# Four column blocks of one input product made in one pass, in a one-core decoder trunk kernel

## The chip, the core and the metric

The kernel runs on one core of a Trainium2 chip. The metric is the device time of one execution in microseconds. Engines are named as the profile names them: PE (TensorE, matmuls), PEld (its weight loads), DVE (VectorE), ACT (ScalarE), POOL (GpSimd), SP (the queue that issues the DMAs).

## What is computed

One layer of a hybrid decoder trunk on 256 positions of width 2048, float32. Around the change only its first part matters: the normalized input times slices of `w_in`, and the compression of two of these slices.

```python
h = rms_norm(x, norm_mix[l])
z = h @ w_in[l]
z_a, z_b, z_cq, z_ckv_c, z_ckv_s, z_ckv_w, z_cg = jnp.split(z, split_at, axis=-1)
...
blocks = jnp.concatenate([sub[:, :, :-1], sub[:, :, 1:]], axis=3) + pos
h = jax.nn.gelu(blocks.reshape(bsz, ng, n_c, CMP_LEN * hd) @ w1)
return h @ w2
```

`z_ckv_c` (512 columns, keys and values to be compressed) and the keys in `z_ckv_s` and `z_ckv_w` (256 each) are the four column blocks of 256 that the change is about. Behind this part come the attentions, an output product, cross attention over a memory, and a squared-ReLU MLP that takes over half of the time.

## The kernel before, in words

Every float32 operand of a large product is split into a high part (rounded to float32r by ScalarE, `split` L82) and a low part (the remainder, by VectorE, L83), and a product is three products of parts. `products_t` (L155 to 175) does one block, 512 rows of the contraction by 256 columns: 8 matmuls of 512 columns (the high weights by both parts of x, L164) and 8 of 256 columns (the low weights by the high part of x, L169). `gemm_t` does a whole product of 256 columns in four such blocks, each with its load, its split and its matmuls. Its sum takes two of the eight PSUM banks; `join` (L191 to 196) adds its two halves on ScalarE and VectorE.

Weights come from memory into five `raw` buffers, all over the one SP queue. The split weights stand in three buffers `wh` and three `wl`, which all products share, the compression's too. PSUM is two pools of four banks each: `pacc` (two sums) and `pmisc`. The rows of an engine run in their order in the program; that order is set by a scheduler when the program is built, which starts from the order in the code.

The order in the code: the first product (`cmps`, L240 to 265) makes both column blocks of `z_ckv_c` together: x comes in pieces, is multiplied by the gains and split (`put_act`, into `hx`), and each block of x meets two weight blocks. Then comes k0 (the selected keys) as a `gemm_t` of its own, with the generator `squares` between its blocks, which joins the first product and sums the squares of x. From that sum come `rx` (the row scale: `mean_eps`, `rstd`; matmul `pss`, L117, POOL's power, L123) and `rxb`, the same along the free axis (`along_free`, matmul `psb`, L133, copy L134). The joined first product (`kraw`, in `cw`) is multiplied by `rxb` (L313), and the generator `compress` (L328 to 371) adds the position term (L330), splits the result into `blk`, and runs `ph`, 64 small matmuls (L340 to 343) in four blocks for the keys, then as many for the values. It is advanced between the blocks of k1 (the window keys) and of sg (`gemm`, 8 blocks of 12 matmuls of 280 columns, L212). Then come wv, cq and the rest.

## Time and profile before

| | |
|---|---|
| runs | 1197.72, 1197.37, 1196.21 us; median 1197.37 |
| profiled execution | 1196.66 us, of which 1194.9 are the span from the first to the last instruction |
| mean granted TensorE clock | 0.999 |
| PE, DVE, ACT, POOL busy | 1178.7, 741.2, 590.4, 12.0 us |
| memory traffic | 224.24 MB, 188 GB/s in the mean |

A row of the timeline gives the start, the busy time, the engine, the line of the code, the operation, the tiles written and read, their shape, and how many like ones follow each other; in brackets stands the idle time before it and what ended it. Matmuls overlap their neighbours' ends, so of two rows of PE the difference of the starts tells the pace, not the busy time.

### The profile page before, as it was taken

What the parts mean: (1) busy time and instruction counts of PE and PEld (TensorE: products, weight loads), DVE (VectorE), ACT (ScalarE), POOL (GpSimd) and SP (SyncE); (2) the same over time, 40 slices, a digit from 0 to 9 for tenths busy, and PEclk for the clock granted to TensorE, in tenths of its full rate; (3) what the DMA queues carried; (4) which work ended last, traced back from release to release, by engine and by line L of the source; (5) the groups of instructions that cost most, each with busy time, mean ns of one, the idle gap of its engine ahead of it and who ended that gap; (6) DMA issues with size and microseconds to landing.
All of it is one profiled execution on the core that took longest, in us unless ns stands there. A gap on an engine that the chain in (4) does not pass through costs nothing.

```text
span 1194.9 us, 16486 instructions
## 1 busy us (share of the span) xinstructions
PE 1178.7 (99%) x6450; PEld 1016.8 (85%) x6450; DVE 741.2 (62%) x938; ACT 590.4 (49%) x812; POOL 12.0 (1%) x18
## 2 busy tenths in 40 slices
PE   8999999999999999999999999999999999999996
PEld 6898888888888889888888888888888888888885
DVE  7875876569776567665545565545566445656554
ACT  7564555466544467544433444433444333444443
POOL 0000000000000000000000000000000000000000
PEclk9999999999999999999999999999999999999999
DMA  8676444557555554555565565556665656565553
GB/s 297 225 256 186 132 124 140 179 183 229 181 190 193 180 174 160 178 192 189 193 192 192 188 190 193 191 193 192 190 189 182 202 193 197 178 193 193 193 179 106
DMA packets 65673, 224.24 MB, mean 188 GB/s; under 512 B 7995, under 2 KB 9531, under 8 KB 65467
## 3 DMA queue, kind: packets, MB, share of 16 engines
q1 hardware_dynamic: 65307, 222.14, 57.6%
q8 instruction: 50, 0.82, 0.3%
q10 hardware_dynamic: 288, 1.05, 0.3%
q14 instruction: 28, 0.23, 0.1%
HBM read 221.06 MB, written 2.10 MB: 187 GB/s over the span
## 4 chain that ended last, share of the span: by engine, by line
PE 96%; DVE 1%; issue 1%; ACT 1%; DMA 1%; SPq 0%; POOLq 0%; POOL 0%; DVEq 0%; ACTq 0%
PE dn L212 27%; PE up L164 20%; PE up L169 10%; PE wo L164 5%; PE cq L164 3%; PE wo L169 2%; PE xo L153 2%; PE v L212 2%; PE bv L212 2%; PE mv L212 2%; PE cmp L164 1%; PE k L164 1%; PE cq L169 1%; PE bq L164 1%; PE xq L164 1%; PE mk L164 1%
## 5 line engine op out<-in xcount | busy, mean ns | idle before, releaser
L83 DVE TENSOR_TENSOR wl<-raw,wh 128x1024 fp32r<-128x1024 f32 (+3 forms) x414 | 496.4, 1201 | 332.2 <-ACT wh L82 329.8
L82 ACT ACTIVATE wh<-raw 128x1024 fp32r<-128x1024 f32 (+3 forms) x414 | 429.0, 1038 | 432.2 <-PE dn L212 185.5
L164 PE MATMUL up<-h,wh 128*128 128x512 f32 x1024 | 316.9, 395 | 0.0
L212 PE MATMUL dn<-wh,hid 128*128 128x512 f32 x992 | 306.2, 389 | 0.0
L169 PEld LDWEIGHTS up<-h,wl 128*128 128x128 f32 x1024 | 187.6, 188 | 42.2
L212 PEld LDWEIGHTS dn<-wh,hid 128*128 128x128 f32 x992 | 186.2, 188 | 38.7
L169 PE MATMUL up<-h,wl 128*128 128x256 f32 x1024 | 197.0, 279 | 0.0
L212 PE MATMUL dn<-wl,hid 128*128 128x512 f32 x496 | 193.3, 390 | 1.1 <-DVE wl L83 0.6
L164 PEld LDWEIGHTS up<-h,wh 128*128 128x128 f32 x1024 | 158.4, 189 | 2.7
L212 PEld LDWEIGHTS dn<-wl,hid 128*128 128x128 f32 x496 | 93.1, 188 | 21.4 <-DVE wl L83 2.2
L164 PE MATMUL wo<-mix,wh 128*128 128x512 f32 x256 | 79.1, 395 | 0.0
L169 PEld LDWEIGHTS wo<-mix,wl 128*128 128x128 f32 x256 | 46.5, 188 | 10.3
L193 ACT ACTIVATE half<-up 128x512 f32<-128x512 f32 x32 | 19.2, 599 | 63.6 <-PE up L164 63.6
L195 DVE TENSOR_TENSOR half<-up,half 128x512 f32<-128x512 f32 x32 | 22.2, 693 | 43.5 <-ACT half L193 43.5
L169 PE MATMUL wo<-mix,wl 128*128 128x256 f32 x256 | 49.0, 279 | 0.0
L164 PE MATMUL cq<-hx,wh 128*128 128x512 f32 x128 | 40.4, 396 | 0.0
L164 PEld LDWEIGHTS wo<-mix,wh 128*128 128x128 f32 x256 | 39.7, 189 | 0.8
L667 DVE SCALAR_TENSOR_TENSOR xt<-dn,m,xt 128x512 f32<-128x512 f32 (+1 forms) x34 | 22.9, 715 | 14.5 <-PE dn L212 14.5
L82 ACT ACTIVATE hid<-half 128x512 fp32r<-128x512 f32 x32 | 20.2, 633 | 16.6 <-DVE half L718 16.6
L169 PEld LDWEIGHTS cq<-hx,wl 128*128 128x128 f32 x128 | 23.5, 188 | 5.1
L164 PE MATMUL cmp<-hx,wh 128*128 128x512 f32 x64 | 21.8, 439 | 5.6 <-ACT wh L82 5.6
L169 PE MATMUL cq<-hx,wl 128*128 128x256 f32 x128 | 25.7, 281 | 0.0
(283 smaller groups left out, 1277.3 us busy)
## 6 DMA issues: line engine op xcount, KB each, us to landing
raw<-in_w_up SPq DMA_DIRECT2D x128, 512.0 KB, 4.3
raw<-in_w_down SPq DMA_DIRECT2D x128, 512.0 KB, 4.4
raw<-in_w_t SPq DMA_DIRECT2D x52, 512.0 KB, 4.0
raw<-in_w_out SPq DMA_DIRECT2D x32, 512.0 KB, 3.8
raw<-in_w_bv SPq DMA_DIRECT2D x8, 512.0 KB, 3.7
raw<-in_w_v SPq DMA_DIRECT2D x8, 512.0 KB, 3.7
raw<-in_w_mk SPq DMA_DIRECT2D x8, 512.0 KB, 4.3
raw<-in_w_q SPq DMA_DIRECT2D x8, 512.0 KB, 4.3
```

The costliest lines, as they stand in the source:

```text
L82: nc.scalar.activation(hi, src, AF.Copy)
L83: nc.vector.tensor_tensor(lo, src, f32(hi), op=ALU.subtract)
L153: nc.tensor.matmul(acc[:, f, 0, :], w[:, kk, fs], x[:, kk, l, :], start=(kk == 0 and j == 0), stop=(kk == 3 and j == 2))
L164: nc.tensor.matmul(acc[:, f].rearrange("p a s -> p (a s)"), wh[:, kk, f * P:(f + 1) * P], xk, start=start, stop=stop)
L169: nc.tensor.matmul(acc[:, f, 0, :], wl[:, kk, f * P:(f + 1) * P], x[:, kk, 0, :], start=False, stop=False)
L193: nc.scalar.activation(lo, acc[:, :, 1, :], AF.Copy)
L195: nc.vector.tensor_tensor(d, acc[:, :, 0, :], lo, op=ALU.add)
L212: nc.tensor.matmul(acc[t][:, :n], lhs[k // 4][:, k % 4, l, ts], w[:, kk, :], start=(k == 0 and j == 0), stop=(k == KD - 1 and j == 2))
L667: nc.vector.scalar_tensor_tensor(xs, acc[t][:, cs], r3[:, t:t + 1], xs, op0=ALU.mult, op1=ALU.add)
```

## The change

All four column blocks are made in one pass over x, in four sums that fill the eight PSUM banks (a pool `first`, closed before `pmisc` and `pacc` are opened). For the first block of x three weight blocks come in pieces beside x's pieces and the fourth whole; for the other three blocks of x the four weight blocks come whole, one after the other. The squares of x lie between them. All four sums are joined behind the last product; `rx`, `rxb` and the compression follow there. There is no product k1 beside which the compression could run: `cgen` is now advanced between the blocks of sg, wv and, if anything were left, cq. The PSUM pools get `reuse_waits="tile"`: a new tile waits for the earlier tiles in its own banks, not for the whole earlier pool.

```diff
--- before.py
+++ after.py
@@ -48,8 +48,6 @@
     wp = ctx.enter_context(tc.tile_pool(name="wp", bufs=3))
     ap = ctx.enter_context(tc.tile_pool(name="ap", bufs=4))
     sp = ctx.enter_context(tc.tile_pool(name="sp", bufs=2))
-    pacc = ctx.enter_context(tc.tile_pool(name="pacc", bufs=2, space=PSUM))
-    pmisc = ctx.enter_context(tc.tile_pool(name="pmisc", bufs=2, space=PSUM))
 
     def f32(t):
         return t.bitcast(F32)
@@ -237,32 +235,6 @@
 
     hx = new_act("hA", "hx")
 
-    cmps = [pacc.tile([P, 2, 2, S], F32, tag="acc", name=f"cmp{m}") for m in range(2)]
-    for b in range(4):
-        ws = []
-        for m in range(2):
-            raw = wp.tile([P, 1024], F32, tag="raw", bufs=5, name="raw")
-            wh = wp.tile([P, 1024], F32R, tag="wh", name="wh")
-            wl = wp.tile([P, 1024], F32R, tag="wl", name="wl")
-            ws.append((raw, wh, wl))
-        i = 0
-        for step in ((1, 1, 2), (2, 2), (4,), (4,))[b]:
-            k = 4 * b + i
-            cs = slice(i * 256, (i + step) * 256)
-            for m, (raw, wh, wl) in enumerate(ws):
-                if m == 0:
-                    nc.sync.dma_start(xres[:, k:k + step, :],
-                                      a["xT"][b].rearrange("p (k s) -> p k s", k=4)[:, i:i + step, :])
-                    if k == 0:
-                        nc.sync.dma_start(gT, a["gT"])
-                loads.append(nc.sync.dma_start(raw[:, cs], a["w_t"][CMP + m, b][:, cs]))
-                if m == 0:
-                    put_act(hx, k, xres[:, k:k + step, :], 0)
-                split(wh[:, cs], wl[:, cs], raw[:, cs])
-            i += step
-        for m, (raw, wh, wl) in enumerate(ws):
-            products_t(cmps[m], hx[b], wh.rearrange("p (k n) -> p k n", k=4), wl.rearrange("p (k n) -> p k n", k=4),
-                       b == 0, b == 3)
     C = {}
 
     def consts(them):
@@ -272,27 +244,68 @@
             with tc.issue_after(loads[-1].ins):
                 nc.sync.dma_start(C[name], a[name].partition_broadcast(P) if name == "bs" else a[name])
 
-    consts([("ident", [P, P]), ("posT", [P, LCMP]), ("sel", [2 * M2, M2]), ("hmask", [P, 4]), ("rowv", [P, 2])])
-    ident = C["ident"]
-
     cw = slot("hC", "cw", F32).rearrange("p k a s -> p (k a s)")
     kraw = cw[:, :4 * S].rearrange("p (g s) -> p g s", g=4)
+    ssq = sp.tile([P, 2, S], F32, tag="ssq", name="ssq")
+
+    with tc.tile_pool(name="first", bufs=1, space=PSUM, reuse_waits="tile") as pfirst:
+        accs = [pfirst.tile([P, 2, 2, S], F32, tag=f"a{m}", name=f"cmp{m}" if m < 2 else f"k{m - 2}") for m in range(4)]
+        cols = [CMP, CMP + 1, KV, KV + 1]
+
+        def load_x(k, n):
+            b = k // 4
+            nc.sync.dma_start(xres[:, k:k + n, :],
+                              a["xT"][b].rearrange("p (k s) -> p k s", k=4)[:, k % 4:k % 4 + n, :])
+
+        def load_w(m, b, raw, cs):
+            loads.append(nc.sync.dma_start(raw[:, cs], a["w_t"][cols[m], b][:, cs]))
+
+        def add_block(m, b, w):
+            products_t(accs[m], hx[b], *(t.rearrange("p (k n) -> p k n", k=4) for t in w), b == 0, b == 3)
+
+        ws = [[wp.tile([P, 1024], F32, tag="raw", bufs=5, name="raw")]
+              + [wp.tile([P, 1024], F32R, tag=n, name=n) for n in ("wh", "wl")] for m in range(3)]
+        k = 0
+        for n in (1, 1, 2):
+            cs = slice(k * 256, (k + n) * 256)
+            load_x(k, n)
+            if k == 0:
+                nc.sync.dma_start(gT, a["gT"])
+            for m in range(3):
+                load_w(m, 0, ws[m][0], cs)
+                if m == 0:
+                    put_act(hx, k, xres[:, k:k + n, :], 0)
+                raw, wh, wl = ws[m]
+                split(wh[:, cs], wl[:, cs], raw[:, cs])
+            k += n
+        for m in range(3):
+            add_block(m, 0, ws[m][1:])
+        w = split_w(load_raw(a["w_t"][cols[3], 0]))
+        add_block(3, 0, w)
+        for b in range(1, 4):
+            for i in range(2):
+                load_x(4 * b + 2 * i, 2)
+                put_act(hx, 4 * b + 2 * i, xres[:, 4 * b + 2 * i:4 * b + 2 * i + 2, :], 0)
+            for m in range(4):
+                w = split_w(load_raw(a["w_t"][cols[m], b]))
+                add_block(m, b, w)
+                for n in {1: (0, None, 1, None), 2: (2, None, 3, None), 3: (4, 5, 6, 7)}[b][m:m + 1]:
+                    if n is not None:
+                        add_squares(ssq, xres[:, 2 * n:2 * n + 2, :], n == 0)
+            if b == 2:
+                consts([("ident", [P, P]), ("posT", [P, LCMP]), ("sel", [2 * M2, M2]), ("hmask", [P, 4]), ("rowv", [P, 2])])
+                ident = C["ident"]
+        k01 = []
+        for m in range(4):
+            j = join(accs[m], "first", kraw[:, 2 * m:2 * m + 2, :] if m < 2 else None)
+            if m >= 2:
+                k01.append(j)
+    pmisc = ctx.enter_context(tc.tile_pool(name="pmisc", bufs=2, space=PSUM, reuse_waits="tile"))
+    pacc = ctx.enter_context(tc.tile_pool(name="pacc", bufs=2, space=PSUM, reuse_waits="tile"))
     vs = slot("hC", "vs", F32).rearrange("p k a s -> p (k a s)")
     vcat = vs[:, :1024].rearrange("p (b t n) -> p b t n", b=2, t=2)
     zb = vs[:, 1024:].rearrange("p (t n) -> p t n", t=2)
     kcat = slot("hB", "kcat").rearrange("p (g a) b s -> p g a b s", g=2)
-    ssq = sp.tile([P, 2, S], F32, tag="ssq", name="ssq")
-
-    def squares():
-
-        for m, acc in enumerate(cmps):
-            join(acc, "cmp", kraw[:, 2 * m:2 * m + 2, :])
-        for b in range(4):
-            for n in (2 * b, 2 * b + 1):
-                add_squares(ssq, xres[:, 2 * n:2 * n + 2, :], n == 0)
-            yield
-
-    acc_k0 = gemm_t(hx, a["w_t"][KV], "k0", between=squares())
     rx = rstd(mean_eps(ssq, "mx"), "rx")
     rxb = along_free(rx, "rxb")
     rq = cp.tile([P, 2], F32, name="rq")
@@ -302,8 +315,8 @@
     consts([("cau", [P, S]), ("mcmp", [P, 2, NCMP]), ("mB", [P, 384]), ("bs", [P, NB]), ("triu", [P, P])])
     cau, mB, mcmp = C["cau"], C["mB"], C["mcmp"]
 
-    def join_split(acc, hi, lo, name, rb=None):
-        j = join(acc, name)
+    def join_split(acc, hi, lo, name, rb=None, joined=False):
+        j = acc if joined else join(acc, name)
         if rb is not None:
             nc.vector.tensor_tensor(j, j, rb[:, None, :].to_broadcast([P, 2, S]), op=ALU.mult)
         split(hi, lo, j)
@@ -311,7 +324,8 @@
     for m in range(2):
         km = kraw[:, 2 * m:2 * m + 2, :]
         nc.vector.tensor_tensor(km, km, rxb[:, None, :].to_broadcast([P, 2, S]), op=ALU.mult)
-    join_split(acc_k0, kcat[:, :, 0, 0, :], kcat[:, :, 1, 0, :], "k0", rxb)
+    for g in range(2):
+        join_split(k01[g], kcat[:, :, 0, g, :], kcat[:, :, 1, g, :], f"k{g}", rxb, joined=True)
 
 
 
@@ -371,9 +385,6 @@
             yield
 
     cgen = compress()
-    acc = gemm_t(hx, a["w_t"][KV + 1], "k1", between=cgen)
-    join_split(acc, kcat[:, :, 0, 1, :], kcat[:, :, 1, 1, :], "k1", rxb)
-
 
     gate = cp.tile([P, 2, 8, 3], F32, name="gate")
     acc = gemm(hx, a["w_sg"], 2, NG, "sg", between=cgen)
@@ -386,9 +397,7 @@
 
     nc.vector.tensor_tensor(gate[:, :, :, 0], gate[:, :, :, 0], C["rowv"][:, :, None].to_broadcast([P, 2, 8]),
                             op=ALU.mult)
-    for _ in cgen:
-        pass
-    acc = gemm(hx, a["w_wv"], 4, S, "wv")
+    acc = gemm(hx, a["w_wv"], 4, S, "wv", between=cgen)
     for t in range(2):
         nc.scalar.activation(vcat[:, 1, t, :], acc[t][:, :S], AF.Copy, scale=rx[:, t:t + 1])
 
@@ -436,8 +445,10 @@
         qT = slot(("hB", "hC")[g], f"q{g}")
         mix[2 + g] = slot("hB", f"mix{2 + g}")
         for m in range(2):
-            acc = gemm_t(hx, a["w_t"][CQ + 2 * g + m], f"cq{g}{m}")
+            acc = gemm_t(hx, a["w_t"][CQ + 2 * g + m], f"cq{g}{m}", between=cgen)
             join_split(acc, qT[:, 2 * m:2 * m + 2, 0, :], qT[:, 2 * m:2 * m + 2, 1, :], "q")
+        for _ in cgen:
+            pass
 
         psc = pmisc.tile([P, 2, 4, 2, NCMP], F32, tag="sc", name="psc")
         for t in range(2):
```

TensorE's order changes only up to the first cq product; behind it its rows are the same. TensorE where the compression begins, before (`k_494` is k1, `ph` the compression, `hx_80` the first block of x):

```order
L164 MATMUL k_494<-hx_80,wh 128x512 x2
L169 MATMUL k_494<-hx_80,wl 128x256 x2
L340 MATMUL ph<-wh,blk 60x128
L341 MATMUL ph<-wl,blk 30x128 x2
L343 MATMUL ph<-wh,blk 60x128
L341 MATMUL ph<-wl,blk 30x128
L343 MATMUL ph<-wh,blk 60x128
L341 MATMUL ph<-wl,blk 30x128
```

The first `ph` stands behind one block of k1, and k1's next block follows after 15 more matmuls of `ph`. TensorE now, at the end of the four products (`k_86` is k1):

```order
L162 MATMUL k_86<-hx_77,wh 128x512 x2
L115 MATMUL pss<-ones,ssq 128x1 x2
L210 MATMUL sg<-wh,hx_74 128x280
L210 MATMUL sg<-wl,hx_74 128x280
L210 MATMUL sg<-wh,hx_74 128x280 x2
```

`pss`, which stood inside the first product, is behind the last one, and sg's 24 matmuls on `hx_74`, two blocks, follow. TensorE after these 24, up to the first `ph` (`hx_75` is the second block of x):

```order
L131 MATMUL psb<-dg,ones 128x128 x2
L210 MATMUL sg<-wh,hx_75 128x280
L210 MATMUL sg<-wl,hx_75 128x280
L210 MATMUL sg<-wh,hx_75 128x280 x2
L210 MATMUL sg<-wl,hx_75 128x280
L210 MATMUL sg<-wh,hx_75 128x280 x2
L210 MATMUL sg<-wl,hx_75 128x280
L210 MATMUL sg<-wh,hx_75 128x280 x2
L210 MATMUL sg<-wl,hx_75 128x280
L210 MATMUL sg<-wh,hx_75 128x280
L354 MATMUL ph<-wh,blk 60x128
L355 MATMUL ph<-wl,blk 30x128 x2
```

After the third sg block 48 `ph` matmuls stand in one piece, and the fourth sg block behind them. VectorE from the row scale to `blk`, before:

```order
L132 TENSOR_SCALAR dg<-ident,rx 128x128 x2
L299 TENSOR_SCALAR rq<-rx 128x2
L301 TENSOR_SCALAR nrx<-rx 128x2
L83 TENSOR_TENSOR wl<-raw,wh 128x1024
L195 TENSOR_TENSOR cw<-cmp_85,half 128x512
L83 TENSOR_TENSOR wl<-raw,wh 128x1024 x2
L313 TENSOR_TENSOR cw<-cw,rxb 128x512 x2
L330 TENSOR_TENSOR cw<-cw,posT 128x32x15 x2
L83 TENSOR_TENSOR wl<-raw,wh 128x1024
L83 TENSOR_TENSOR blk<-cw,blk 128x32x30
L83 TENSOR_TENSOR wl<-raw,wh 128x1024
```

VectorE at the same place now:

```order
L116 TENSOR_SCALAR mx<-pss 128x2
L130 TENSOR_SCALAR dg<-ident,rx 128x128 x2
L312 TENSOR_SCALAR rq<-rx 128x2
L314 TENSOR_SCALAR nrx<-rx 128x2
L81 TENSOR_TENSOR wl<-raw,wh 128x1024
L81 TENSOR_TENSOR wl<-raw,wh 128x560
L326 TENSOR_TENSOR cw<-cw,rxb 128x512 x2
L321 TENSOR_TENSOR half<-half,rxb 128x512 x2
L344 TENSOR_TENSOR cw<-cw,posT 128x32x15 x2
L81 TENSOR_TENSOR wl<-raw,wh 128x1024
L81 TENSOR_TENSOR kcat<-half,kcat 128x2x256 x2
L81 TENSOR_TENSOR blk<-cw,blk 128x32x30
```

The scaling of two k blocks (L321) and two low parts of `kcat` are new between `dg` and the low part of `blk` (the last row); of four `wl` of 1024 columns and a join, two `wl` of 1024 and one of 560 are left there. On ScalarE two table loads are added, one before the values' gelu and one before the first exponential of the attentions.

## Rows read from the trace of the kernel before

**Rows 1.** The page, busy time of TensorE, its share of the span, instructions.
```profile
PE 1178.7 (99%) x6450; PEld 1016.8 (85%) x6450; DVE 741.2 (62%) x938; ACT 590.4 (49%) x812; POOL 12.0 (1%) x18
```

**Rows 2.** The page, chain that ended last, shares by engine.
```profile
PE 96%; DVE 1%; issue 1%; ACT 1%; DMA 1%; SPq 0%; POOLq 0%; POOL 0%; DVEq 0%; ACTq 0%
```

**Rows 3.** TensorE's waits, whole span: us in total, times, longest.
```profile
PE cmp L164 <- ACT wh L82: 5.6, 3, 4.4
PE ox L651 <- DVE oT L83: 0.7, 1, 0.7
```

**Rows 4.** Timeline of PE in the first product.
```profile
4.44 2.08 PE L164 MATMUL cmp<-hx,wh 128*128 128x512 f32 x4 [4.44 <-ACT wh L82]
...
6.31 1.06 PE L169 MATMUL cmp<-hx,wl 128*128 128x256 f32 x4
...
12.25 0.62 PE L164 MATMUL cmp<-hx,wh 128*128 128x512 f32 x2
...
18.57 0.40 PE L169 MATMUL cmp<-hx,wl 128*128 128x256 f32 x2
19.89 0.73 PE L164 MATMUL cmp<-hx,wh 128*128 128x512 f32 x2 [0.92 <-ACT wh L82]
...
21.41 0.40 PE L169 MATMUL cmp<-hx,wl 128*128 128x256 f32 x2
...
32.14 0.62 PE L164 MATMUL k<-hx,wh 128*128 128x512 f32 x2
```

**Rows 5.** Chain of waits in order of time (start, us), two later steady products.
```profile
512.11 0.93 PE up L164 x4
...
523.27 0.93 PE up L164 x4
```

**Rows 6.** Timeline of ScalarE and VectorE, from the row scale to blk.
```profile
29.54 0.60 ACT L193 ACTIVATE half<-cmp 128x512 f32<-128x512 f32 x1 [2.44 <-PE cmp L164]
...
29.88 0.16 DVE L118 TENSOR_SCALAR mx<-pss 128x2 f32<-128x2 f32 x1 [0.83 <-PE pss L117]
...
30.87 0.48 DVE L132 TENSOR_SCALAR dg<-ident,rx 128x128 f32<-128x128 f32 x2
...
31.41 1.22 DVE L83 TENSOR_TENSOR wl<-raw,wh 128x1024 fp32r<-128x1024 f32 x1
...
37.14 1.29 DVE L313 TENSOR_TENSOR cw<-cw,rxb 128x512 f32<-128x512 f32 x2
...
38.35 1.93 DVE L330 TENSOR_TENSOR cw<-cw,posT 128x480 f32<-128x480 f32 x2
...
40.30 1.02 ACT L82 ACTIVATE blk<-cw 128x960 fp32r<-128x960 f32 x1 [1.10 <-DVE cw L330]
...
41.36 1.16 DVE L83 TENSOR_TENSOR blk<-cw,blk 128x960 fp32r<-128x960 f32 x1
```

**Rows 7.** Timeline of PE: pss, psb, the first ph, and six matmuls of sg.
```profile
29.34 0.50 PE L117 MATMUL pss<-ones,ssq 128*128 128x1 f32 x4
...
35.40 0.60 PE L133 MATMUL psb<-dg,ones 128*128 128x128 f32 x4
...
46.52 0.22 PE L340 MATMUL ph<-wh,blk 128*60 128x128 f32 x1
...
62.05 0.29 PE L212 MATMUL sg<-wl,hx 128*128 128x280 f32 x1
...
62.43 0.29 PE L212 MATMUL sg<-wl,hx 128*128 128x280 f32 x1
```

**Rows 8.** Groups of VectorE, 0 to 130 us: busy us, mean ns | idle.
```profile
L83 DVE TENSOR_TENSOR wl<-raw,wh 128x560 fp32r<-128x560 f32 x8 | 5.9, 736 | 0.3 <-ACT wh L82 0.3
...
L83 DVE TENSOR_TENSOR kcat<-half,kcat 128x512 fp32r<-128x512 f32 x2 | 1.4, 689 | 0.4 <-ACT kcat L82 0.4
```

**Rows 9.** Groups of ScalarE, 0 to 130 us: a table load.
```profile
L355 ACT ACT_TABLE_LOAD x1 | 1.3, 1283 | 0.0
```

**Rows 10.** The page, granted TensorE clock in 40 slices, tenths.
```profile
PEclk9999999999999999999999999999999999999999
```

## The prediction

> **What bounds the kernel now.** I read the busy shares first: TensorE (PE) is busy for 99% of the span [rows 1]. A busy PE need not be at its pace, so I read the chain of waits next: 96% of what ended last is PE [rows 2]. So the kernel lasts as long as TensorE's instructions in their written order, plus the holes in that order. The list of TensorE's waits shows where the holes are: the first product waits 5.6 us for its weights, 4.4 of them before the first matmul, and no other line waits more than 0.7 us [rows 3]. The timeline of TensorE then gives the first product piece by piece [rows 4], and a steady product gives the pace to hold it against: 11.16 us, from one product's first matmuls to the next's, with four 512-column matmuls in 0.93 us [rows 5]. That is 0.2325 for one of these and, with 32 of each kind in a product, 0.116 for a 256-column one.
>
> The first product (two column pairs, so two steady products' work, 22.33 us) takes from 4.44 to 32.14, that is 27.70 us [rows 4]. With some 0.4 us for the small pss matmuls in it, 5.0 us are lost there. At first four 512-column matmuls take 1.87 us (4.44 to 6.31), twice the steady 0.93: the lower of the two clock levels, 1.2 GHz. By 12.25 fourteen matmuls of either kind are done (counted in the timeline between the rows), worth 14 x 0.349 = 4.89 us at full pace, in 7.81: **2.9 us** go to the slow start. The rest, **2.1 us**, lies mostly between 18.57 and 21.41, where two short and four long matmuls (1.16 us of work) take 2.84 because the splits of the weights come late (0.92 us of it is shown as a wait for ScalarE's wh) [rows 4].
>
> **The change, part by part.** I call T0 the moment when TensorE ends the last of the four products.
>
> *1. One product of four.* The 64 steps of the four products are the same matmuls; none is added. What can go is the 2.1 us of late splits: for each block of x TensorE now has two weight blocks more, 2 x 2.79 = 5.58 us of cover, and VectorE only two splits more, 2 x 1.22 us [rows 5, 6]. But the third and fourth blocks of x still put their own splits and squares ahead of weights on the same two engines. Bounds: gain 0 to 2.1; I take 1.5, since the added cover is over twice the added work. The slow start stays: the first matmul waits for the same first pieces (xT, gT, one weight piece), and the third weight piece stands behind these on SP's queue. The constants, moved behind the third block of x, are needed only after T0 and cost nothing.
>
> *2. What came behind the products.* Before, sum of squares, rx, rxb, the scaling of kraw and the making of blk lay beside k0 and k1: pss stands at 29.34 and ph at 46.52, 17.2 us later, and TensorE had product work all the way [rows 7]. Now pss stands behind the last product, and until the first ph TensorE has pss (0.50), three blocks of sg and psb (0.60); a block of sg is 12 matmuls, three in 0.38 us [rows 7], so 4.6 us for three, **5.7 us** in all. Behind that the written order has 48 ph matmuls in a row, and none can begin before both halves of blk are there. TensorE takes matmuls as written, so the later sg cannot pass them; the three weight buffers hold compression weights by then in any case.
>
> When is blk there? I follow the order of VectorE (the last fence under the change) with the durations of before [rows 6, 8]:
> - join of the last product: ScalarE starts 0.2 after T0 (as its join at 29.54 after the product that ends where pss stands, 29.34 [rows 7]) and takes 0.60; VectorE's add takes 0.69, as kcat's row of the same size: T0 + 1.5
> - wl of the second sg block, 0.74: T0 + 2.2
> - mx 0.16, then rx on POOL, until dg can start (29.88 to 30.87): 1.0: T0 + 3.2
> - dg, rq and nrx (30.87 to 31.41): 0.54: T0 + 3.8
> - wl of a compression block 1.22 and of the third sg block 0.74: T0 + 5.7 (psb and rxb are done beside these)
> - cw by rxb 1.29; k0 and k1 by rxb, two more of 128x512 at 0.69: T0 + 8.4
> - kraw and posT into cw, 1.93: T0 + 10.3
> - another wl 1.22, two low parts of kcat 1.38: T0 + 12.9 (ScalarE's half of blk, 1.02, is done by then)
> - the low half of blk 1.16: **T0 + 14.1**
>
> So TensorE stands still for 14.1 - 5.7 = **8.4 us** between T0 and the first ph, part of it before the third sg block (its wl is done only at T0 + 5.7) and some 7 in one piece in front of ph. Of the chain's 14.1 us, 6.7 are work that ph does not need but that stands ahead on VectorE (wl, k0 and k1, kcat). Bounds: 7.4 if VectorE's small ones and the semaphores overlap by another microsecond, 9.4 if each hand-over costs a little more.
>
> *3. Behind the wait.* The compression's second half now lies beside sg and wv. No matmul is added. ScalarE gets two more table loads (1.28 us each [rows 9]), because gelu now comes after the exponentials of the gates. ScalarE has slack; if they hit a split that TensorE waits for, 2.6 us. Bounds 0 to 2.6; I take 0.4. The loads run ahead during the wait, until the five raw buffers are full, so none is late behind it. The new release rule of the PSUM pools waits tile by tile; sg's first matmul needs a join that ends before T0, so nothing.
>
> *4. The clock.* Nothing in the trace of before stops TensorE for more than 0.7 us after the start [rows 3], so whether its clock falls in a wait of 7 us is not shown. The nearest row is the start: after 4.44 us without a matmul the engine ran at half pace, at a cost of 2.9 us [rows 4]. Bounds 0 to 2.9; I take 2.0, as the new hole is longer than that one and as some of the slow stretch will hide behind splits that are late anyway. The Trainium skill ("TensorE: Matmul & The Clock Gate", Part 1 and the section on HAM oscillation) says that a long idle gap puts the array back to 1.2 GHz until it has been busy again for a while; by that rule the term is there for certain, and without the rule, with the holes of 0.7 us as the only evidence after the start, the sum would be 2.0 less.
>
> **Sum:** -1.5 + 8.4 + 0.4 + 2.0 = +9.3 us. The profiled execution took 1196.66, so its like would be 1206.0; the median of the runs is 0.7 above it, 1197.37, which gives **1206.7**. A measurement of this kernel tells 0.2% (2.4 us) from no change.
>
> **The rivals.**
> - *The wait is there, the clock does not fall.* Then 1206.7 - 2.0 = 1204.7. For it: the granted clock of before is at its top in every slice of the page [rows 10] and shows no fall anywhere, not even in the slow start. Against it: the start's pace itself [rows 4].
> - *The wait is mostly covered.* If VectorE's instructions overlap far more than their rows say, so that blk is there at about T0 + 8, the wait is 2.3, the clock stays, and 2.3 + 0.4 - 1.5 gives 1198.6: no difference that can be told. Against it: the long rows follow each other at their full duration (37.14 + 1.29 is 38.43, and the next began at 38.35 [rows 6]).
> - *Faster: the first product gives back its loss and no wait replaces it.* Place: the start and ph. With a third product the engine is denser in its first microseconds; if that ended the slow stretch half way, 1.4 of the 2.9 go, with the 2.1 of late splits 3.5, so 1193.9. It decides from the point at which the wait in front of ph is under about 1 us, that is, when blk is there by T0 + 6.7, or when ph is not in fact held by blk's low half. Against it: the chain has eight steps of VectorE in a row that cannot pass each other.
>
> **How the numbers follow.** The forecast with the fall of the clock 0.52, without it 0.36, covered wait 0.07, faster 0.05. The first two differ by 2 us and are both slower by more than 2.4. Low end: full gain 2.1, wait 7.4, nothing else, +5.3, 1202.7; I go to 1201.8 to take in a part of the third case. High end: gain 0.5, wait 9.4, 1.5 behind it, clock 2.9, +13.3, which is all bad ends at once; 1211.5 leaves it out. Faster 0.05, same 0.07, slower 0.88.
>
> **What would show it.** Right: the PE timeline has the four products end at about 4.44 + 44.66 + 2.9 + 0.6 = 52.6; the list of waits names ph, waiting for VectorE's blk, at some 7 us, near 60 to 67 us; TensorE's idle time in that stretch is 8 to 9 us; everything from the cq products on is as before, only later. Step 1 is wrong if the first product still has waits of 2 us between 15 and 45. Step 4 is right if the matmuls behind the wait take twice their steady time. The prediction is wrong if ph starts within 7 us of T0, or if the later stages grow too.

## The result, and the profile after

The changed kernel takes 1206.52 us (median of 6 runs, 1205.35 to 1207.0), the kernel before 1196.78 (6 runs): a ratio of 1.0079 with a 95% interval of 1.0069 to 1.0089. The change costs 9.7 us by the medians, and the forecast was 1206.7. The profiled execution took 1206.15 us with a span of 1204.4, against 1196.66 and 1194.9: 9.5 us more.

The page first: TensorE's busy time, its granted clock in 40 slices, and the chain that ended last ([rows 1, 10, 2] before).

```profile
PE 1181.0 (98%) x6450; PEld 1017.8 (85%) x6450; DVE 741.0 (62%) x938; ACT 593.2 (49%) x814; POOL 12.0 (1%) x18
...
PEclk9989999999999999999999999999999999999999
...
PE 94%; DVE 2%; issue 1%; ACT 1%; DMA 1%; SPq 0%; POOL 0%; POOLq 0%; DVEq 0%; ACTq 0%
```

The number of matmuls is the same. VectorE now has 2% of the chain instead of 1%, and in the third slice (60 to 90 us) the granted clock is no longer at its top. TensorE's waits name the place ([rows 3] before; us in total, times, longest):

```profile
PE ph L354 <- DVE blk L81: 6.0, 1, 6.0
PE cmp L162 <- ACT wh L80: 4.7, 2, 4.4
PE wv L210 <- ACT wh L80: 0.7, 1, 0.7
```

A wait of 6.0 us in front of ph is new. TensorE's timeline shows the joined product and what follows it ([rows 4, 7] before):

```profile
4.41 2.07 PE L162 MATMUL cmp<-hx,wh 128*128 128x512 f32 x4 [4.41 <-ACT wh L80]
...
17.08 0.51 PE L167 MATMUL k<-hx,wl 128*128 128x256 f32 x2 [0.53 <-DVE wl L81]
...
24.57 0.63 PE L162 MATMUL cmp<-hx,wh 128*128 128x512 f32 x2
...
53.88 0.50 PE L115 MATMUL pss<-ones,ssq 128*128 128x1 f32 x4
...
59.41 0.40 PE L210 MATMUL sg<-wl,hx 128*128 128x280 f32 x1 [0.46 <-DVE wl L81]
...
67.08 0.33 PE L354 MATMUL ph<-wh,blk 128*60 128x128 f32 x1 [5.99 <-DVE blk L81]
...
67.42 0.31 PE L357 MATMUL ph<-wh,blk 128*60 128x128 f32 x1
67.53 0.31 PE L355 MATMUL ph<-wl,blk 128*30 128x128 f32 x1
...
70.43 0.22 PE L355 MATMUL ph<-wl,blk 128*30 128x128 f32 x1
70.49 0.22 PE L357 MATMUL ph<-wh,blk 128*60 128x128 f32 x1
```

- The four products take 53.88 - 4.41 = 49.47 us. Their work at the steady pace is 44.66 (two times the 22.33 that the prediction has for two), so **4.8 us** are lost in them, where two products lost 5.0 before. All of it is lost before 24.57: at that row 44 long and 44 short matmuls are done, 15.35 us of work in 20.16.
- From T0 = 53.88 to ph at 67.08 are 13.2 us, in which TensorE has 5.3 us of work (pss and psb 0.36 each, three blocks of sg 4.6). It stands still for **7.9 us**, 6.0 of them in one piece in front of ph; most of the rest lies around psb and the third block of sg (0.3 in front of 58.55, 0.46 in front of 59.41).
- The first ph matmuls follow each other in 0.107 us, from 70.4 on in 0.06. Some 29 at the slower pace cost 29 x 0.047 = **1.4 us**.

The stretch windows (us, then each engine's busy time and instructions, then the granted clock, DMA share and GB/s) show the same clock:

```profile
60.00:65.00 5.00, 1.09 (x9) 0.87 (x7) 5.00 (x7) 3.11 (x4) 0.00 (x0) 0.85 0.38 122
65.00:70.00 5.00, 2.92 (x28) 2.95 (x29) 4.09 (x6) 0.67 (x1) 0.00 (x0) 0.50 0.22 59
70.00:75.00 5.00, 5.00 (x59) 4.90 (x58) 3.11 (x4) 3.12 (x6) 0.00 (x0) 0.97 0.51 158
```

A granted clock of 0.50 is the lower level, 1.2 GHz. VectorE's timeline behind T0 shows what ph waited for ([rows 6] before):

```profile
56.95 0.48 DVE L130 TENSOR_SCALAR dg<-ident,rx 128x128 f32<-128x128 f32 x2 [0.82 <-POOL rx L121]
...
57.48 1.87 DVE L81 TENSOR_TENSOR wl<-raw,wh 128x1024 fp32r<-128x1024 f32 x2
59.27 1.29 DVE L326 TENSOR_TENSOR cw<-cw,rxb 128x512 f32<-128x512 f32 x2
60.47 1.28 DVE L321 TENSOR_TENSOR half<-half,rxb 128x512 f32<-128x512 f32 x2
61.68 1.85 DVE L344 TENSOR_TENSOR cw<-cw,posT 128x480 f32<-128x480 f32 x2
63.43 1.23 DVE L81 TENSOR_TENSOR wl<-raw,wh 128x1024 fp32r<-128x1024 f32 x1
64.56 1.30 DVE L81 TENSOR_TENSOR kcat<-half,kcat 128x512 fp32r<-128x512 f32 x2
65.76 1.17 DVE L81 TENSOR_TENSOR blk<-cw,blk 128x960 fp32r<-128x960 f32 x1
```

From 56.95 to 66.93 VectorE does not rest. This chain lay beside k0 and k1 before; now nothing lies beside it but three blocks of sg.

Parts of the difference, in us: products -0.2, standing still +7.9, slow ph +1.4, the wait of wv +0.7, together 9.8. At the first matmul of the output product TensorE is 9.9 us late (`wo`, 282.37 us before and 292.28 now), and at the first of the MLP's second product too (`dn`, 568.25 and 578.17). The spans differ by 0.4 less than that because of the last stage: from the first `dn` to the end the fourteen traces of this document take between 625.7 and 626.7 us, with no order by kernel.

### The profile page after: what moved, and what is told of

Read it like the earlier page. It is cut to its first block, busy times and chain, and to the rows that moved or that the text cites. A ratio compares the mean times of both kernels' runs of the same rounds, so it can differ in the third digit from the quotient of the medians.

```text
span 1204.4 us, 16486 instructions
## 1 busy us (share of the span) xinstructions
PE 1181.0 (98%) x6450; PEld 1017.8 (85%) x6450; DVE 741.0 (62%) x938; ACT 593.2 (49%) x814; POOL 12.0 (1%) x18
## 4 chain that ended last, share of the span: by engine, by line
PE 94%; DVE 2%; issue 1%; ACT 1%; DMA 1%; SPq 0%; POOL 0%; POOLq 0%; DVEq 0%; ACTq 0%
PE dn L210 27%; PE up L162 20%; PE up L167 10%; PE wo L162 5%; PE cq L162 2%; PE wo L167 2%; PE xo L151 2%; PE v L210 2%; PE bv L210 2%; PE mv L210 2%; PE cq L167 1%; PE xq L162 1%; PE bq L162 1%; PE mk L162 1%; PE u L162 1%
```

## The experiments

Twelve kernels ran, four on each of three chips, with runs of the kernel before on each (medians 1197.22, 1197.25 and 1196.99 us). Ratios are to these. The changed kernel itself ran again on the first chip only, so on the other two a kernel is held against it by way of the kernel before.

**The changed kernel again**, as the mark for the others. Measured: 1206.17 us, 9.0 over the kernel before, ratio 1.0079 (1.0067 to 1.0092); ph waits 6.0 us.

> The changed kernel itself, as the measure for the runs beside it. Every theory: 9 to 10 us over the kernel before.

**k0 and k1 behind blk.** Of the chain, the scaling and the splitting of k0 and k1 are not needed by ph. They are held behind blk's low half.

```diff
-    for g in range(2):
-        join_split(k01[g], kcat[:, :, 0, g, :], kcat[:, :, 1, g, :], f"k{g}", rxb, joined=True)
...
     acc = gemm(hx, a["w_sg"], 2, NG, "sg", between=cgen)
+    with tc.issue_after(blo[0].ins):
+        for g in range(2):
+            join_split(k01[g], kcat[:, :, 0, g, :], kcat[:, :, 1, g, :], f"k{g}", rxb, joined=True)
```

> The scaling and splitting of the two k blocks is held behind the low half of blk on VectorE. Theory of the wait, simple form (the chain from the row scale to blk sets the time, one to one): the first ph comes 2.7 us earlier than in the changed kernel, the hole in front of it falls from 6.0 to some 3.3 us, the clock then may stay, and the time is 2.7 to 4.1 us under the changed kernel. Second form (VectorE's whole work after the last product is what is late, not only the chain): the hole in front of ph shrinks as much, but the split for the next sg block is late by most of it, and the time is only 0.3 to 1.0 us under the changed kernel. Rival (the joint product itself costs the time): no change, within 0.3 us.

Measured: 1204.08 us, ratio 1.006 (1.0048 to 1.0073), 2.1 less than the changed kernel. TensorE's timeline:

```profile
64.58 0.33 PE L354 MATMUL ph<-wh,blk 128*60 128x128 f32 x1 [3.62 <-DVE blk L346]
...
66.95 0.31 PE L355 MATMUL ph<-wl,blk 128*30 128x128 f32 x1
...
67.46 0.22 PE L355 MATMUL ph<-wl,blk 128*30 128x128 f32 x1
```

ph waits 2.4 us less, and 2.1 of these arrive in the time: the length of VectorE's chain is paid almost one to one. The time is a little under the range of the first form (2.7 to 4.1 us less) and far over that of the second. That two steps of the chain are not needed there explains a quarter of the loss, not more. The clock falls in the shorter wait too.

**wv ahead of sg.** wv is a product that needs nothing of the chain. It is written ahead of sg without the compression between its blocks; the compression goes beside sg and cq.

```diff
+    acc = gemm(hx, a["w_wv"], 4, S, "wv")
...
     acc = gemm(hx, a["w_sg"], 2, NG, "sg", between=cgen)
...
-    acc = gemm(hx, a["w_wv"], 4, S, "wv", between=cgen)
```

> The product wv (11.5 us of matmuls that need nothing of the row scale) is put between the joint product and sg, the compression beside sg and the first cq product. Theory of the wait: wv covers the chain, the hole in front of ph is under 1.5 us, the granted clock stays full, and the time is 0 to 2.5 us over the kernel before, 7 to 9.5 under the changed one. Rivals (the joint product costs the time by itself, or the compression beside sg with its table loads does): still 7 us or more over the kernel before.

Measured: 1199.15 us, ratio 1.0019 (1.001 to 1.0029). Its waits:

```profile
PE sg L210 <- ACT wh L80: 0.9, 1, 0.9
...
PE ph L354 <- DVE blk L81: 0.3, 1, 0.3
```

With a product beside the chain, the wait for blk shrinks from 6.0 to 0.3 and the granted clock is 1.00 in every 5 us from 60 to 75; 7.0 of the 9 us come back. This shows the cause of the loss: not the chain by itself, but that nothing lay beside it. Small waits of 0.8 and 0.9 us in front of sg, ph and cq are left.

**24 idle matmuls** of 512 columns (5.6 us, results unused) in the stretch behind the products, so that the wait is the same in time but TensorE does not stand still for long.

```diff
...
+            if n == 2:
+                dm = pmisc.tile([P, NB], F32, tag="tr", name="dm")
+                for i in range(24):
+                    nc.tensor.matmul(dm, hx[0][:, 0, 0, :P], hx[0][:, 0].rearrange("p a s -> p (a s)"),
+                                     start=(i == 0), stop=(i == 23))
...
```

> 24 added matmuls of 512 columns (5.6 us) into a PSUM tile that nobody reads stand between the second sg block and the third, so that TensorE has something to do while blk is made; the rest is the changed kernel. Theory of the clock: the first ph comes when it did, within 0.5 us, the granted clock stays full, the ph matmuls behind it take 0.06 us each and not 0.107, and the time is 1.0 to 1.8 us under the changed kernel. Rival (the slow stretch hides behind splits that are late anyway): the clock stays but the time is the same, within 0.4 us.

Measured: 1205.04 us, ratio 1.007 (1.0057 to 1.0082). The median is 1.1 us less than the changed kernel's, inside the range of the theory of the clock, but the trace does not show what that theory said. A wait of 2.1 us was left, ph began at full pace, and it fell to the lower one a microsecond later, for 30 matmuls. The profiled execution was the slowest of the five (1206.35 us), and its span of 1204.6 is that of the changed kernel; whether the clock fell in the four others is not shown.

```profile
67.31 0.24 PE L354 MATMUL ph<-wh,blk 128*60 128x128 f32 x1 [2.08 <-DVE blk L81]
...
68.23 0.22 PE L357 MATMUL ph<-wh,blk 128*60 128x128 f32 x1
...
68.64 0.31 PE L355 MATMUL ph<-wl,blk 128*30 128x128 f32 x1
```

**x behind the fourth weight block.** The second question was why joining gave back only 0.2 us. First guess: the splits of x's second block stand ahead of that of the fourth weight block and wait for x. They are put behind it (`wh3` and `w3` are the two halves of that block's split).

```diff
-                put_act(hx, 4 * b + 2 * i, xres[:, 4 * b + 2 * i:4 * b + 2 * i + 2, :], 0)
+                with tc.issue_after(wh3.ins), tc.issue_after(w3.ins):
+                    put_act(hx, 4 * b + 2 * i, xres[:, 4 * b + 2 * i:4 * b + 2 * i + 2, :], 0)
```

> As the changed kernel, but the splits of x's second, third and fourth block stand, on ScalarE and on VectorE, behind the split of the first x block's fourth weight block. This asks why joining the products gave back only about 0.2 us of the first products' loss (4.8 lost against 5.0 before), where 1.5 had been forecast: the list of TensorE's work between 9.6 and 24.6 us is worth 12.3 us and takes 15.0. Theory A (squares): the scheduler pulls the squares of x ahead of weight splits on both engines (six squares at 0.6 us and their additions at 0.7 us between 9 and 24 us). Then moving x alone changes little: within 0.7 us of the changed kernel, 1205.5 to 1207. Theory B (x ahead of the fourth weight block): the two splits of x that stand ahead of that block's split, waiting until 13.9 us for x, make the lateness. Then the waits of k on wh and wl (0.19 and 0.53) go and 0.7 to 1.5 us come back: 1204.7 to 1205.5.

Measured: 1206.46 us, ratio 1.0077 (1.0063 to 1.009): no change that can be told. pss begins at 53.84. A square of x had taken the place ahead of the split and waited for the same x, so this run alone does not clear x of it.

**Squares behind the weights.** Each square of x is held behind the split of the weight block beside which it is written (`wh` and `wl`); in the changed kernel the scheduler had pulled them forward.

```diff
                     if n is not None:
-                        add_squares(ssq, xres[:, 2 * n:2 * n + 2, :], n == 0)
+                        with tc.issue_after(wh.ins), tc.issue_after(wl.ins):
+                            add_squares(ssq, xres[:, 2 * n:2 * n + 2, :], n == 0)
```

> As the changed kernel, but each square of x and its addition stand, on ScalarE and VectorE, behind the split of the weight block beside which they are written. Theory A (squares ahead of splits): most of the 2.7 us lost between 9.6 and 24.6 us goes, the waits of k and cmp on wl there vanish, pss begins near 52 instead of 53.9, all later stages move with it: 1.0 to 2.5 us less, 1203.7 to 1205.2. Theory B: nothing changes in that stretch, 1206 to 1207. In both the wait of ph for blk stays at about 6 us and the matmuls behind it start at half pace.

Measured: 1205.94 us, ratio 1.007 (1.0057 to 1.0083). pss begins at 53.29, 0.6 earlier: the waits for wl at 20 and 23 us are gone, and behind 17.7 us nothing is lost, where the changed kernel loses 0.9. But by 18 us 4.2 us are lost already, against 3.9. The two traces with held squares lose 4.2 us in the products in all; the nine others with the same loads lose 4.5 to 5.0, so holding the squares is worth 0.3 to 0.8. The rest is lost as before, and ScalarE's timeline says to what:

```profile
11.18 0.63 ACT L80 ACTIVATE wh<-raw 128x512 fp32r<-128x512 f32 x1 [0.84 <-DMA raw<-in_w_t]
12.22 0.63 ACT L80 ACTIVATE wh<-raw 128x512 fp32r<-128x512 f32 x1 [0.42 <-DMA raw<-in_w_t]
14.17 0.91 ACT L85 ACTIVATE hx<-xres,gT 128x256 fp32r<-128x256 f32 x2 [1.31 <-DMA xres<-in_xT]
```

It waits three times in a row for data from memory. Theory A accounts for 0.3 to 0.8 of the 2.7 us, under its forecast of 1.0 to 2.5, and a third theory, the loads, was formed here.

**Two loads less.** The third and fourth weight block for x's first block are not loaded, and the data of the first and second stand in for them; all splits and matmuls stay. So k0 and k1 do not come out as the layer has them, and the two buffers that the loads would take are free sooner.

```diff
-                load_w(m, 0, ws[m][0], cs)
+                if m < 2:
+                    load_w(m, 0, ws[m][0], cs)
...
-                raw, wh, wl = ws[m]
+                raw, wh, wl = ws[m % 2]
+                wh, wl = ws[m][1:]
...
-        w = split_w(load_raw(a["w_t"][cols[3], 0]))
+        w = split_w(ws[1][0])
```

> The changed kernel without the loads of the third and fourth weight block for x's first block: the raw data of the first and second are split again in their place, so that k0 and k1 take their first quarter from the compression's weights. All splits and matmuls remain; 1 MB of the 5.9 MB that are moved in the first 20 us does not. Moving the splits of x (no change) and holding the squares (0.6 us) did not bring back the 2.7 us that the joined product loses between 9.6 and 24.6 us. Theory C (the loads: TensorE, ScalarE and VectorE wait in turn for weights and x that land late, the fourth weight block near 14 us): most of it comes back, pss begins 1.3 to 2.5 us earlier, 51.4 to 52.6, and the time falls to 1203.8 to 1205. Theory D (the splits themselves: ScalarE and VectorE are full from 15 to 25 us): pss stays at 53.3 or over and the time at 1206.

Measured: 1204.85 us, ratio 1.0067 (1.0054 to 1.008).

```profile
14.91 0.73 PE L162 MATMUL k<-hx,wh 128*128 128x512 f32 x2 [0.48 <-ACT wh L80]
15.86 0.74 PE L162 MATMUL cmp<-hx,wh 128*128 128x512 f32 x2 [0.22 <-ACT wh L80]
...
51.76 0.50 PE L115 MATMUL pss<-ones,ssq 128*128 128x1 f32 x4
...
64.95 0.33 PE L356 MATMUL ph<-wh,blk 128*60 128x128 f32 x1 [5.99 <-DVE blk L81]
```

The loss in the products falls from 4.8 to 51.76 - 4.41 - 44.66 = 2.7 us. By 18 us the other eleven traces of the joined product had all lost 3.6 to 4.2 us (counted as above, matmuls done against time gone), this one 2.7, and it loses nothing more behind that. So data that land late cost some 0.9 to 1.5 us in the first 18; with them early, the squares do no harm near 20 either. The 1.2 us between 14 and 17 that stay are lost beside ScalarE's splits, three of them in a row (13.80 to 16.75). Of the 2.1 us gained at T0, 1.1 to 1.3 arrive in the time, as one counts against this chip's kernel before or the mark. In the traces 1.85 of them are still there at the first `wo` (290.43 against 292.28 us), since ph has seven slow matmuls more here (0.3); the rest goes in the last stage, where this trace is one of the longest (626.7 us from `dn` on).

**The compression later.** As wv ahead of sg, with the compression starting only after five blocks of sg.

```diff
+    def later():
+        for _ in range(5):
+            yield
+        yield from compress()
+
-    cgen = compress()
+    cgen = later()
```

> As the run with the wv product moved ahead of sg (1199.15), but the compression starts only after five weight blocks of sg and goes on beside the two cq products, so that between the last of the four products and the first ph TensorE has wv and five blocks of sg, over 20 us against the chain's 13.2. The theory of the wait: ph waits for nothing, the small waits of that run in front of sg, ph and cq (0.9, 0.8, 0.8, because splits of sg and of compression weights came in the same short blocks) go too, and 2 to 4 us come back: 1195.0 to 1197.2, level with the kernel before or a little under it. Rival: the compression costs the cq products what it no longer costs in front, because its weights take turns with theirs in the three buffers; then waits of cq of over 1 us stand in the list and the time stays at 1199 or over.

Measured: 1196.99 us, ratio 0.9999 (0.999 to 1.0008): all of the loss has come back. Of TensorE's waits between the products and the attentions none is left in the list. The rival's waits of cq do not stand in it.

```profile
PE cmp L162 <- ACT wh L80: 5.4, 2, 4.3
PE ox L667 <- DVE oT L81: 0.7, 1, 0.7
```

**32 idle matmuls**, as the 24 above.

> As the changed kernel with 32 idle matmuls of 512 columns (7.4 us) in the stretch between the last product and the first ph, where 24 of them still left a wait of 2.1 us and the granted clock fell behind it. Their result is used nowhere. The theory of the clock (it falls because TensorE stands still in front of ph, and that costs 1.4 us): now no wait of ph over 0.5 us is left, the granted clock stays at 1.00 through 60 to 75 us, ph runs at 0.06 us apart, and 1.0 to 1.5 us come back: 1204.6 to 1205.6. Rival (the fall has another cause than standing still, so that filling does not help): the granted clock falls again between 65 and 75 us and the time is 1206 or over.

Measured: 1205.9 us, ratio 1.0071 (1.0059 to 1.0084). The two windows in which ph runs:

```profile
65.00:70.00 5.00, 4.08 (x46) 3.42 (x44) 4.97 (x7) 3.25 (x4) 0.00 (x0) 1.00 0.02 3
70.00:75.00 5.00, 5.00 (x55) 4.98 (x56) 3.62 (x5) 2.80 (x6) 0.00 (x0) 1.00 0.78 228
```

With 7.4 us of idle matmuls in the hole the clock stays at its top, and ph, which waits 0.2 us, runs at 0.06 us apart. So the fall comes from standing still. But the time hardly moves. The schedule has changed as well: the low part of ph's third weight block is now made behind the next additions of posT, and ph waits 0.7 us for it at 70.00.

This run shows the cause of the fall; its price stands in the traces side by side. Those with the same wait or a longer one differ in how many ph matmuls are slow, the changed kernel's two traces too (29 and 40), and TensorE's time from the first ph to the first wv differs with it:

| trace | slow ph matmuls | first ph to first wv, us |
|---|---|---|
| x behind the fourth weight block | 24 | 14.68 |
| the changed kernel | 29 | 14.92 |
| two loads less | 36 | 15.19 |
| the changed kernel again | 40 | 15.38 |
| a longer chain (the next run) | 41 | 15.46 |

That is 0.046 us for each slow matmul, what its row says: the slow pace is paid in full, 1.1 to 1.9 us here. With 47 slow ones, and slow matmuls of sg behind them, the run with the held squares takes 16.08. The run with 32 idle matmuls has none and takes 14.84, of which 0.7 are its new wait; by the table it would be 14.3, so some 0.6 us of it stay unexplained.

**A longer chain.** Two multiplications by 1.0 more in VectorE's chain, over the window of cw that becomes blk.

```diff
+            if m == 0:
+                for _ in range(2):
+                    nc.vector.tensor_scalar_mul(cw[:, 4 * S:4 * S + LCMP * M2], cw[:, 4 * S:4 * S + LCMP * M2], 1.0)
             split(blk[:, :, :M2], blk[:, :, M2:], win.rearrange("p l g n -> p l (g n)"))
```

> The changed kernel with two more VectorE multiplications by 1.0 over the window in cw (128x960), between the additions of posT and the splitting of blk, so that VectorE's chain from the last product to blk is longer by two instructions of 0.6 to 1.1 us. The theory (that chain sets when ph begins, and TensorE has nothing else to do): the wait of ph and the time grow by just what the two instructions take: ph waits 7.2 to 8.2 us, the time is 1207.2 to 1208.9. Rival (the time is set by something else that ends at the same moment, the loads or the weight splits behind the chain): ph waits longer but the time stays within 0.5 us of the changed kernel.

Measured: 1208.97 us, ratio 1.0097 (1.0082 to 1.0113); the span is 1207.2, 2.8 more than that of the changed kernel.

```profile
65.34 0.65 DVE L348 TENSOR_SCALAR cw<-cw 128x960 f32<-128x960 f32 x1
...
66.51 0.65 DVE L348 TENSOR_SCALAR cw<-cw 128x960 f32<-128x960 f32 x1
68.23 1.16 DVE L81 TENSOR_TENSOR blk<-cw,blk 128x960 fp32r<-128x960 f32 x1 [1.07 <-ACT blk L80]
...
69.54 0.33 PE L357 MATMUL ph<-wh,blk 128*60 128x128 f32 x1 [8.29 <-DVE blk L81]
```

The two take 0.6 us each, but ph waits 2.3 us more: ScalarE's half of blk, which had lain beside VectorE's work (63.56 to 64.58 in the changed kernel), can begin only behind them, and VectorE waits 1.07 for it. The chain runs over two engines, and so wait and time came out just over the forecast (7.2 to 8.2 and 1207.2 to 1208.9). The remaining 0.5 of the 2.8 is mostly the clock: ph runs at the slower pace until 74.0, 12 matmuls longer than in the changed kernel's trace, 12 x 0.047 = 0.6 us. That part is not shown to come from the longer chain, as the changed kernel's other trace has 40 slow matmuls without it. The rival, that something else ends at the same moment, has fallen.

**The best of both**: compression later and squares behind the weights.

> The run with the late compression (1196.99, level with the kernel before) with the squares of x held behind the weight splits as well. Holding the squares alone made pss begin 0.6 us earlier (53.29 against 53.88), because TensorE's two waits for wl near 20 and 23 us went. With the wait of ph gone there is nothing behind to swallow that: 0.3 to 1.0 us less, 1196.0 to 1196.7, the best of the study. Rival (what is gained in the first products is lost behind them, as in the run with the squares alone, which came out 0.5 under the changed kernel at most): 1197 or over.

Measured: 1196.42 us, ratio 0.9994 (0.9985 to 1.0003). pss begins at 53.31. The time is 0.6 us under its chip's kernel before, where the run with the later compression alone was 0.3 under; the ratio's interval takes in 1, so the difference from the kernel before cannot be told. It is not shown that the gain at T0 reaches the end: a cq product now waits 1.1 us for its split, and the first `dn` matmul stands at 568.74 us, at 567.98 in the run without held squares.

**The kernel before with the later compression**: two products, k0, k1, then wv, sg, and the compression from the sixth block of sg on.

> The kernel before, with its two first products and k0, k1 as they were, but with the order behind them of the late compression: wv ahead of sg, the compression from the sixth weight block of sg on and beside the cq products. It asks what the joined product is worth by itself, once nothing waits behind it. Theory (the joined product is worth next to nothing: its loss at the start is 4.8 us against 5.0): within 1 us of the run with the late compression, 1196.3 to 1198.0. Rival (joining is worth its late splits, and the late compression has a cost of its own that hides this): this kernel then shows that cost bare and is at 1198 or over.

Measured: 1197.53 us, ratio 1.0004 (0.9995 to 1.0012). It is 1.1 us above the best joined kernel on the same chip. The intervals of the two ratios overlap, but the eleven times of each, held against each other directly, give means 1.0 us apart (95% interval 0.4 to 1.7), so a small difference is likely there. That kernel has its squares held and this one has not, so the difference is not the worth of joining alone. The joined kernel with unheld squares ran on another chip, 0.3 under its kernel before, where this one is 0.5 over. So joining is worth between nothing and about 1 us, and neither the order behind it nor the joining shows a hidden cost.

## Why the prediction came out

The time, 1206.52 against 1206.7, and the mechanism were right. That the number came so close is luck: the terms were off by +1.3, -0.5, +0.3 and -0.6, which nearly cancels, and the base of the forecast, 1197.37 from three runs, lies 0.6 over the median of all six. The sum with all bad ends, 1210.7, lies inside the stated range, which was said to leave it out.

*1. One product of four: forecast -1.5, measured -0.2.* This is the step that failed. It held that five more microseconds of matmuls beside each block of x would cover the late splits. The sign that it set for this came: between 15 and 24.6 us 2.1 us are still lost. It counted the two engines' work and not the loads. TensorE's rows of before name only late splits, but ScalarE's rows and the windows of the same trace show late data and full DMA engines (the last two figures are their busy share and GB/s):

```profile
5.49 0.51 ACT L87 ACTIVATE hx<-xres,gT 128x256 fp32r<-128x256 f32 x1 [0.70 <-DMA xres<-in_xT]
...
5.00:10.00 5.00, 5.00 (x17) 4.30 (x16) 3.59 (x8) 4.05 (x9) 0.00 (x0) 1.00 0.93 257
10.00:15.00 5.00, 5.00 (x26) 3.92 (x26) 4.47 (x10) 4.33 (x10) 0.00 (x0) 1.00 1.01 379
```

Between 4 and 16 us ScalarE waits 2.1 us for x and weights there, and 3.5 in the changed kernel. In the joined product TensorE loses 2.7 us between 9.6 and 24.6: some 1 to loads, some 0.6 to squares that the scheduler pulled forward, the rest near 15 us at the fourth weight block. The slow start, said to stay at 2.9, cost 2.1 here up to 9.6 us; counted to 12.3 us, as the 2.9 were, 2.7 are lost, the rest of them to a late split. Over the eleven traces with the same loads the slow start cost 1.4 to 2.7 us, and yet by 18 us the loss was 3.6 to 4.2 in each: where the slow start was short, TensorE waited the longer for data. So the slow stretch can end early, as the rival of the faster kernel has it, and that is worth next to nothing while the data are late. That a denser start is what ends it is not shown: kernels with the same first matmuls had it both short and long.

*2. What came behind the products: forecast 8.4 us of standing still, measured 7.9.* T0 came at 53.88 instead of 52.6 (1.3 of it from step 1), ph at T0 + 13.2 instead of 14.1, the place and the releaser as said. Each step of the chain came in the order that the sum has it, but the long rows overlap: the next begins about 0.1 us before the one before it ends, so that cw by rxb, 1.29 in its row, takes 1.20 of the chain, and over some ten rows this makes the 0.9. The lower bound allowed for a microsecond of overlap, though among the small instructions. The prediction's own pair of rows showed it: 37.14 + 1.29 is 38.43, and the next row began at 38.35, which is not the full duration. TensorE's own work was 0.4 smaller than forecast, as pss and psb take 0.36 each from start to start and not their rows' 0.50 and 0.60. And of the 6.7 us of the chain that were called work that ph does not need, the two low parts of compression weights, 2.4 us, belong to ph's second and third weight block, which stand in the same 48 matmuls.

*3. Behind the wait: forecast 0.4, measured 0.7.* wv waits 0.7 us at 86.79 for ScalarE's wh. The size was about right, the reason was not. The table load that stands ahead of these splits is that of the gates, which the kernel before has too (at 77.75 us, L382). What is new is the place: the gates' work now comes while splits for the compression and for wv take turns. The first of the two added loads is the one at 96.25, the second comes at 123.92, and TensorE waits for neither.

```profile
82.74 1.28 ACT L393 ACT_TABLE_LOAD   x1
...
84.73 2.96 ACT L80 ACTIVATE wh<-raw 128x1024 fp32r<-128x1024 f32 x3
...
96.25 1.28 ACT L379 ACT_TABLE_LOAD   x1
```

*4. The clock: forecast 2.0, measured 1.4.* It fell, as the windows and the pace of ph show, and it did not fall where TensorE had a product or the 32 idle matmuls in the hole. The Trainium skill ("TensorE: Matmul & The Clock Gate", the section on HAM oscillation) says that a long idle gap puts the array back to the lower clock. The granted clock of 0.50 behind the 6.0 us agrees. What sets the price is not the length of the hole against that of the start, by which the size was taken, but how long the clock stays low after work has come back: here from 67.1 to 70.3 us. At the same wait of 6.0 us the five traces that have it show 24 to 47 slow ph matmuls, that is 1.1 to 2.2 us, so that 1.4 is one draw of several, and 2.0 would have been another.

The rivals: the wait without a fall of the clock (1204.7) is excluded by the windows. The covered wait (1198.6) did not come, as VectorE's rows overlap by 0.1 us and not by six; the run with wv ahead of sg (1199.15) comes near its time in another way, with a product over the same chain. The faster kernel did not come: the first products kept their loss, and blk was there 13.2 us behind T0.

## What to carry to other kernels

Where a step is moved off the path of a bound engine, ask what will lie beside the chain that follows it: here 13 us of VectorE's and ScalarE's work had been free beside two products and cost 7.9 us of standing still when the two products were pulled in front of it. The remedy was not to shorten the chain (two steps less gave 2.1 us) but to put independent products beside it (7.0 us, and all of it with the compression started later). And before crediting a longer product with covering late splits, look whether the splits themselves wait for loads.

## What was not expected of the hardware

- The clock can fall after work has come back: with 2.1 us of standing still, ph ran at 0.06 us apart for a microsecond and only then at 0.107, until 71.6. Behind waits of 3.6 us and more ph had the lower clock at once.
- After the same wait of 6.0 us the clock stayed low for 24 to 47 ph matmuls, in two traces of the same kernel for 29 and 40. One trace does not give the price of a fall.
- In the slow start the granted clock is given as 1.00 (all windows to 60 us), although four 512-column matmuls take 1.87 us (4.41 to 6.28), twice their steady 0.93. At ph the granted clock and the pace agree. A clock of 1.00 in the first microseconds does not prove the full pace; the spacing of the matmuls does.
